# A decoder trunk on one core: the first half's inverses ahead of the convolution columns, the second half's convolution one stage sooner

## The chip, the core and the metric

The kernel runs on one core of a Trainium2 chip. The metric is the device time of one execution in microseconds; the time of a version is the median of several runs. Engines are called TensorE (PE in the rows; PEld is its loading of weights), VectorE (DVE), ScalarE (ACT), GpSimd (POOL) and SyncE (SP, which here only issues transfers).

## What is computed

One layer of a decoder with 1024 tokens of 1024 features, all in fp32. Three sub-layers, each `x <- x + RMSNorm_post(f(RMSNorm_pre(x)))`:

```python
# 1. mixer: one input projection p = h @ w_in, whose columns are split
y_conv = silu(layer_norm(causal_conv31(u * sigmoid(v)) ))   # 512 channels, 31 taps each
y_rwkv = rwkv7(...)                                         # 8 heads of 64, a recurrence over tokens
x = x + rms(concat(y_conv, y_rwkv) @ w_out)
# 2. cross attention of 4 heads into 256 memory tokens
x = x + rms(softmax(q @ km.T) @ vm @ wo)
# 3. SwiGLU
x = x + rms((silu(gu[:F]) * gu[F:]) @ w_down)
```

The recurrence per head keeps a 64 x 64 state S:

```python
s_kk = S @ kk_t
S = S * w_t - outer(s_kk, kk_t * a_t) + outer(v_t, k_t)
y_t = S @ r_t
```

## The kernel before, in words

The tokens are worked in two halves (b = 0 and 1) of 512. Every fp32 matmul is made of three: a weight tile of 128 x 1024 comes by SP into one of four `wraw` buffers (L174), ScalarE rounds it to a high part `whi` (L167) and VectorE takes the rest `wlo` (L168), each with two buffers; activations are split into `ahi` and `alo` in the same way. `mm3` (L190 to L192) does high times high, low times high and high times low, so 24 matmuls of 512 columns use one weight tile.

A half goes through these stages:

- **w_in_block** (L291): the input projection, panel by panel. Four panels are the convolution's (`conv_cols`); their gated result `evh` (L322) is stored to the DRAM array `hd`. The others (`mix_cols`) belong to the recurrence.
- **rwkv_prep** (L408): decays, keys and the products inside chunks of 64 tokens.
- **rwkv_values** (L558; its transposes are `psv`, L568) and **rwkv_inverse** (L578): a triangular inverse of 64 x 64 matrices, 32 x 32 blocks at first: 31 dependent steps of two VectorE instructions (L603, L604) on `Tt`. Through the DRAM arrays sc2 and sc3 the blocks come back in another layout, and matmuls `psx` (L623) and `pst2` (L630) finish `TT`.
- **rwkv_chain** (L634): 8 chunks, one after another. Each has five groups of 16 small matmuls on TensorE: psp (L671), psq (L676), psu (L681), pss (L686), psy (L696). Between them ScalarE copies (`pt`, `uv`) and VectorE updates the state `Sn` (L688 to L693). After two chunks `rwkv_out` (L707) normalizes the output with sums of heads on TensorE (`psbs`, L404) and a root on ScalarE and stores `Y` to `yd`.
- **conv** (L327): for each of four panels of channels a row `hin` of 542 tokens is loaded from `hd` (two buffers), ScalarE does the first tap (L340) and VectorE 30 more (L342), one instruction of 512 columns each, adding to `acc`: 120 taps a half. Then `conv_norm` (L347): layer norm and silu, the result stored to `yd`.
- **mix_out** (L796): `load_split` (L728) reads `yd` back and splits it, and 16 weight tiles make the output projection, `pst`.
- **attention** (L851), and **ffn** (L888).

`run` (L936) writes the stages in program order. `weave(main, side, rate)` (L51) mixes two generators by the microseconds that they yield; `self.fill(us)` lets the generator in `self.filler` write some of its work where the stage written now has gaps. Tile pools are stacks on two sides of the on-chip memory (`push`, `pop`); a pool pushed after another was popped takes over its space, and its first writers wait for that tile's last readers. The program is then put in order for each engine by the scheduler of the tile framework from this writing order and its own estimates, so the final order of an engine can be read only from the built program. An engine's list is fixed after that.

Before the change, in the first half: after the prep the convolution's four panels are projected; the convolution's pool is pushed under the inverse's, so its taps can run during the inverse; the recurrence is written, then the projection of the memory tokens (`memory_maps`), the norm of the second half and its first panels, woven with the convolution. Then mix_out and attention of the first half with the second half's other panels as filler. In the second half the recurrence has FFN0, the feed-forward block of the first half, as filler, woven with the second convolution.

Of the kernel before, what the change touches and what calls it, by code (L numbers as in the profile page):

```python
# [50 lines left out]
def weave(main, side, rate):  # L51

    lag = 0.0
    for us in main:
        yield us
        lag += us * rate
        while lag > 0.0:
            lag -= next(side, 1e9)
    drain(side)


def drain(*gens):
    for g in gens:
        for _ in g:
            pass


class Trunk:
# [867 lines left out]
    def run(self):  # L936
        tc = self.tc
        L, R = "left", "right"
        opened = {}

        def push(name, side):
            opened[name] = tc.tile_pool(name=name, bufs=1, side=side, reuse_waits="tile")
            return opened[name].__enter__()

        def pop(*names):
            for n in names:
                opened.pop(n).__exit__(None, None, None)


        self.fl = dict(res0=6.0, load0=6.0, soft0=5.0, res1=5.0, load1=16.0, soft1=0.0)  # L950
        self.filler = None
        self.credit = 0.0
        conv_cols, mix_cols = (4, 0, 6, 2), (20, 12, 8, 16, 14, 10, 18)

        edge = push("edge", R).tile([P, 56], F32, name="edge")
        self.nc.gpsimd.memset(edge, 0.0)

        a1 = push("a1", R)
        ev = push("ev", R)
        mk = push("mk", R)  # L960
        a0 = push("a0", R)
        h0, h1, mT = self.pairs(a0), self.pairs(a1), self.pairs(mk, MEM, "m")
        self.xn = 4
        self.xp = push("xa", L)
        self.normed(self.x, 0, (0, 4), h0, "g_mix", 2)
        drain(self.w_in_block(0, h0, ev, mix_cols[:1], 2))
        self.normed(self.mem, 0, (0, 2), mT, "g_mem", 2)
        pop("xa")
        self.lora_split(ev)
        self.nc.scalar.dma_start(out=self.hd[:, 0:CONVW - 1].rearrange("(j p) t -> p j t", p=P), in_=self.state[:, :, 0:CONVW - 1])  # L970
        drain(self.w_in_block(0, h0, ev, mix_cols[1:4]))
        pp = push("prep0", L)
        prep = self.rwkv_prep(0, pp)
        next(prep)
        drain(self.w_in_block(0, h0, ev, mix_cols[4:]))
        drain(prep)
        pop("prep0")
        drain(self.w_in_block(0, h0, ev, conv_cols))
        pop("a0")
        kv = push("kv", R)  # L980
        tp = push("tt0", L)
        TT = tp.tile([P, NCH * HP, CH], F32, tag="TT", name="TT")
        kp = push("conv0", L)
        pp = push("inv0", L)
        self.rwkv_values(0, pp)
        self.rwkv_inverse(0, pp, TT)
        self.xn = 2
        self.xp = push("xb", R)
        pop("inv0")

        gp = push("gn0", L)
        mp = push("mix0", L)
        self.rwkv_chain(0, mp, gp, TT)
        def next_norm():
            for t in range(0, 4, 2):
                self.normed(self.x, TB, (t, t + 2), h1, "g_mix", 2, (self.pd, "d"))
                yield 1.0 * 2
        maps = self.memory_maps(mT, ev, kv)
        w1 = self.w_in_block(1, h1, ev, conv_cols)
        main = chain(islice(maps, 16), next_norm(), islice(w1, 0), maps, w1)  # L1000
        drain(weave(main, self.conv(0, kp), 1.0))
        pop("mix0", "gn0", "conv0", "tt0", "xb", "kv", "mk")
        self.filler = self.w_in_block(1, h1, ev, mix_cols)

        yp = push("y0", L)
        a2 = push("a2", L)
        self.xn = 3
        self.xp = push("xc", R)
        ap = push("pc", R)
        drain(self.mix_out(0, a2, yp))  # L1010
        drain(self.attention(0, self.nextT, a2, yp, ap))
        self.fill(1e9)
        pop("pc", "xc")
        pop("ev", "a1")

        ya, ss = self.ya_tiles(yp), self.sums()
        fp = push("f0", L)
        self.filler = self.ffn(self.nextT, ya, ss, fp)
        pp = push("prep1", R)
        drain(self.rwkv_prep(1, pp))  # L1020
        pop("prep1")
        tp = push("tt1", R)
        TT = tp.tile([P, NCH * HP, CH], F32, tag="TT", name="TT")
        kp = push("conv1", R)
        pp = push("inv1", R)
        self.rwkv_values(1, pp)
        self.rwkv_inverse(1, pp, TT)
        pop("inv1")
        gp = push("gn1", R)
        mp = push("mix1", R)  # L1030
        self.rwkv_chain(1, mp, gp, TT)
        side = self.conv(1, kp)
        self.filler = weave(self.filler, side, 1.5)
        self.fill(270.0)
        drain(side)
        pop("mix1", "gn1", "conv1", "tt1")
        a3 = push("a3", R)
        y1 = push("y1", R)
        self.xn = 3
        self.xp = push("xd", R)  # L1040
        ap = push("pd1", R)
        drain(self.mix_out(1, a3, y1))
        drain(self.attention(1, self.nextT, a3, y1, ap))
        self.fill(1e9)
        drain(self.residual(0, ya, ss, 2, self.x2d, self.out, None, None))
        pop("pd1", "xd")
        pop("f0", "a2", "y0")

        ya, ss = self.ya_tiles(y1), self.sums()
        fp = push("f1", L)  # L1050
        self.wq, self.wbufs = push("we", L), 4
        self.xn = 5
        self.xp = push("xe", L)
        drain(self.ffn(self.nextT, ya, ss, fp))
        drain(self.residual(1, ya, ss, 2, self.x2d, self.out, None, None))
        pop("xe")
        pop("we")
        pop("f1")
        pop("y1", "a3", "edge")
# [54 lines left out]
```

## Time and profile before

| | |
|---|---|
| median of 3 runs | 1652.2 us (1651.72 to 1656.0) |
| the profiled execution | 1650.82 us, of it span 1649.1 us |
| TensorE busy | 1534.7 us (93%) |
| VectorE busy | 1065.5 us (65%) |
| ScalarE busy | 687.2 us (42%) |
| GpSimd busy | 51.0 us (3%) |
| mean granted clock of TensorE | 0.956 |

The page gives the busy time of each engine; a span is what lies between the first and the last instruction of the profiled execution. The busy shares are averages over stages of different kinds: the page's second part, the span in 40 slices, has TensorE at 9 tenths or more nearly everywhere, with dips at slices 5 to 7 (7 each), 10 and 11 (7 and 5) and 25 to 27 (7, 5 and 8). A slice is 41.2 us long. The last two dips are the recurrences of the two halves.

### The profile page before, as it was taken

Reading aid. Unit: us, or ns where it says so; the run is one execution under the profiler, and the core shown is the slowest. Engines: PE = TensorE matmul, PEld = TensorE weight load, DVE = VectorE, ACT = ScalarE, POOL = GpSimd, SP = SyncE. Lnnn points to the kernel's source line nnn. Section 1 sums busy time; section 2 is a strip of 40 time slices with the busy share of each in tenths; the row PEclk is TensorE's granted clock in tenths of the full one; section 3 lists DMA queues with packets and bytes.
Section 4 is the critical chain, followed back from the end, with each engine's and each line's share of the span. In section 5 each row is a group of like instructions: output and inputs, shape, how many; then the busy total and the mean of one; then the engine's idle time right before and its main releaser. Section 6 shows DMA issues by size and latency. Waiting matters only on the chain. (4 is left out here: it accounts for less than half of the span.)

```text
span 1649.1 us, 22648 instructions
## 1 busy us (share of the span) xinstructions
PE 1534.7 (93%) x8688; PEld 1258.7 (76%) x8688; DVE 1065.5 (65%) x1702; ACT 687.2 (42%) x1062; POOL 51.0 (3%) x102
## 2 busy tenths in 40 slices
PE   7999777997599999999999997589999999999997
PEld 6787766876487888787888886478887788888886
DVE  5678699986445646768799986446547634344445
ACT  5654454556434434654222246534435332222222
POOL 1000100000000000000000000001001100000000
PEclk9999997998599999999999997689999999999999
DMA  5576993846336235457833345445226623333321
GB/s 207 169 228 203 306 303 118 260 151 218 105 125 215 96 106 192 145 171 216 252 121 112 94 129 179 129 134 204 90 90 210 249 90 97 97 100 94 98 90 51
DMA packets 175643, 257.36 MB, mean 156 GB/s; under 512 B 68912, under 2 KB 110000, under 8 KB 175536
## 3 DMA queue, kind: packets, MB, share of 16 engines
q1 hardware_dynamic: 174576, 255.08, 48.8%
q8 instruction: 68, 1.11, 0.3%
q10 hardware_dynamic: 960, 0.85, 0.2%
q14 instruction: 39, 0.32, 0.1%
HBM read 196.58 MB, written 59.31 MB: 155 GB/s over the span
## 5 line engine op out<-in xcount | busy, mean ns | idle before, releaser
L167 ACT CAST whi<-wraw 128x1024 fp32r<-128x1024 f32 x256 | 268.5, 1050 | 593.3 <-PE psf L191 242.8
L168 DVE TENSOR_TENSOR wlo<-wraw,whi 128x1024 fp32r<-128x1024 f32 x256 | 313.0, 1224 | 282.6 <-ACT whi L167 281.3
L192 PE MATMUL psf<-ahi,wlo 128*128 128x512 f32 (+1 forms) x1200 | 456.0, 381 | 5.1 <-DVE wlo L168 5.0
L190 PE MATMUL psf<-ahi,whi 128*128 128x512 f32 (+1 forms) x1200 | 454.7, 380 | 5.6 <-ACT whi L167 4.6
L191 PE MATMUL psf<-alo,whi 128*128 128x512 f32 (+1 forms) x1200 | 455.2, 380 | 0.0
L190 PEld LDWEIGHTS psf<-ahi,whi 128*128 128x128 f32 x1200 | 228.1, 190 | 49.7 <-ACT whi L167 6.4
L192 PEld LDWEIGHTS psf<-ahi,wlo 128*128 128x128 f32 x1200 | 227.8, 190 | 49.6 <-DVE wlo L168 7.4
L191 PEld LDWEIGHTS psf<-alo,whi 128*128 128x128 f32 x1200 | 228.1, 190 | 42.0 <-issue 1.2
L342 DVE SCALAR_TENSOR_TENSOR acc<-hin,cols,acc 128x512 f32<-128x512 f32 x240 | 171.4, 749 | 1.7 <-ACT acc L340 1.6
L190 PE MATMUL pst<-whi,ahi 128*128 128x512 f32 x384 | 139.6, 403 | 16.8 <-ACT ahi L167 14.8
L191 PE MATMUL pst<-wlo,ahi 128*128 128x512 f32 x384 | 151.9, 397 | 0.0
L192 PE MATMUL pst<-whi,alo 128*128 128x512 f32 x384 | 147.1, 395 | 2.4 <-DVE alo L168 2.4
L191 PE MATMUL pst<-wlo,fhi 128*128 128x512 f32 x352 | 137.4, 391 | 0.0
L192 PE MATMUL pst<-whi,flo 128*128 128x512 f32 x352 | 134.3, 390 | 0.0
L190 PE MATMUL pst<-whi,fhi 128*128 128x512 f32 x352 | 133.3, 393 | 0.0
L190 PEld LDWEIGHTS pst<-whi,ahi 128*128 128x128 f32 x384 | 73.3, 192 | 33.0 <-ACT ahi L167 15.8
L192 PEld LDWEIGHTS pst<-whi,alo 128*128 128x128 f32 x384 | 72.6, 191 | 18.1 <-DVE alo L168 3.1
L191 PEld LDWEIGHTS pst<-wlo,ahi 128*128 128x128 f32 x384 | 73.9, 192 | 15.1
L191 PEld LDWEIGHTS pst<-wlo,fhi 128*128 128x128 f32 x352 | 66.1, 188 | 14.3 <-DVE wlo L168 0.4
L190 PEld LDWEIGHTS pst<-whi,fhi 128*128 128x128 f32 x352 | 65.8, 188 | 14.3 <-ACT whi L167 0.4
L192 PEld LDWEIGHTS pst<-whi,flo 128*128 128x128 f32 x352 | 66.1, 188 | 13.6
L230 POOL TENSOR_TENSOR rstd<-rstd,mhalf 128x1 f32<-128x1 f32 x50 | 35.4, 717 | 1314.1 <-DVE rstd L229 1304.6
(236 smaller groups left out, 1688.3 us busy)
## 6 DMA issues: line engine op xcount, KB each, us to landing
wraw<-in_w_gu_dram SPq DMA_DIRECT2D x88, 512.0 KB, 3.6
wraw<-in_w_in_dram SPq DMA_DIRECT2D x44, 512.0 KB, 4.0
wraw<-in_w_down_dram SPq DMA_DIRECT2D x44, 512.0 KB, 3.5
wraw<-in_wkv_dram SPq DMA_DIRECT2D x16, 512.0 KB, 5.4
am<-amd SPq DMA_DIRECT2D x16, 512.0 KB, 5.2
wraw<-in_w_out_dram SPq DMA_DIRECT2D x16, 512.0 KB, 3.9
wraw<-gd SPq DMA_DIRECT2D x16, 512.0 KB, 4.3
wraw<-vwd SPq DMA_DIRECT2D x16, 512.0 KB, 3.3
```

The source lines that it names most:

```text
L167: self.nc.scalar.copy(out=hi, in_=src)
L168: self.nc.vector.tensor_tensor(out=lo, in0=src, in1=hi.bitcast(F32), op=ALU.subtract)
L190: mm(ps, w[0], x[0], start=start, stop=False)
L191: mm(ps, w[0], x[1], start=False, stop=False)
L192: mm(ps, w[1], x[0], start=False, stop=stop)
L230: nc.gpsimd.tensor_tensor(r, r, self.mhalf, op=ALU.pow)
L342: nc.vector.scalar_tensor_tensor(out=a, in0=h[:, k:k + TB], scalar=w(k), in1=a, op0=ALU.mult, op1=ALU.add)
```

## The change

Three edits in `run`. First, the values and inverse of the first half (pools tt0 and inv0) are written ahead of the projection of the convolution's four panels, and the pool of the first convolution is pushed after inv0 has been popped, so that its tiles take over the inverse's space. Second, the pool of the second convolution is pushed before the first half's output projection, and that projection and the attention, as one generator, are woven with the second convolution at a rate of 0.7. Third, the second half's recurrence has only FFN0 as filler.

```diff
--- before.py
+++ after.py
@@ -975,18 +975,18 @@
         drain(self.w_in_block(0, h0, ev, mix_cols[4:]))
         drain(prep)
         pop("prep0")
-        drain(self.w_in_block(0, h0, ev, conv_cols))
-        pop("a0")
-        kv = push("kv", R)
+
         tp = push("tt0", L)
         TT = tp.tile([P, NCH * HP, CH], F32, tag="TT", name="TT")
-        kp = push("conv0", L)
         pp = push("inv0", L)
         self.rwkv_values(0, pp)
         self.rwkv_inverse(0, pp, TT)
+        drain(self.w_in_block(0, h0, ev, conv_cols))
+        pop("inv0", "a0")
+        kv = push("kv", R)
         self.xn = 2
         self.xp = push("xb", R)
-        pop("inv0")
+        kp = push("conv0", L)
 
         gp = push("gn0", L)
         mp = push("mix0", L)
@@ -1007,10 +1007,13 @@
         self.xn = 3
         self.xp = push("xc", R)
         ap = push("pc", R)
-        drain(self.mix_out(0, a2, yp))
-        drain(self.attention(0, self.nextT, a2, yp, ap))
+        kp = push("conv1", R)
+        def blocks():
+            yield from self.mix_out(0, a2, yp)
+            yield from self.attention(0, self.nextT, a2, yp, ap)
+        drain(weave(blocks(), self.conv(1, kp), 0.7))
         self.fill(1e9)
-        pop("pc", "xc")
+        pop("conv1", "pc", "xc")
         pop("ev", "a1")
 
         ya, ss = self.ya_tiles(yp), self.sums()
@@ -1021,7 +1024,6 @@
         pop("prep1")
         tp = push("tt1", R)
         TT = tp.tile([P, NCH * HP, CH], F32, tag="TT", name="TT")
-        kp = push("conv1", R)
         pp = push("inv1", R)
         self.rwkv_values(1, pp)
         self.rwkv_inverse(1, pp, TT)
@@ -1029,11 +1031,8 @@
         gp = push("gn1", R)
         mp = push("mix1", R)
         self.rwkv_chain(1, mp, gp, TT)
-        side = self.conv(1, kp)
-        self.filler = weave(self.filler, side, 1.5)
         self.fill(270.0)
-        drain(side)
-        pop("mix1", "gn1", "conv1", "tt1")
+        pop("mix1", "gn1", "tt1")
         a3 = push("a3", R)
         y1 = push("y1", R)
         self.xn = 3
```

The names in the rows below carry the program's buffer numbers: acc_2696 is the first half's convolution, acc_4446 the second's; hin_2697, 2937, 3212 and 3553 are the rows of the first's four panels, hin_4447, 4766, 5239 and 5436 those of the second's.

VectorE in the changed program, in the midst of the first half's recurrence (L724 is its output):

```order
L240 SCALAR_TENSOR_TENSOR yrr_2418<-ysq_2410,yrr_2418 128x512
L351 TENSOR_TENSOR lnsa_3819<-acc_2696 128x512
L342 SCALAR_TENSOR_TENSOR acc_4446<-hin_4447,cols_77,acc_4446 128x512
L342 SCALAR_TENSOR_TENSOR acc_2696<-hin_3212,cols_77,acc_2696 128x512
L724 TENSOR_TENSOR Y_2250<-Y_2250,yrr_2418 128x512
L342 SCALAR_TENSOR_TENSOR acc_4446<-hin_4447,cols_77,acc_4446 128x512
L342 SCALAR_TENSOR_TENSOR acc_2696<-hin_3553,cols_77,acc_2696 128x512
```

Before, only the first convolution's taps stood here; the second's begin beside its third and fourth panels, and go on alternating with them until the first convolution's taps end.

VectorE at the first alo of the first half's output projection; alo comes from araw, the row read back from `yd`. Before:

```order
L721 TENSOR_SCALAR yrr_2650<-psbs_2647 128x512
L239 SCALAR_TENSOR_TENSOR ysq_2642<-ysq_2642,yrr_2650 128x512
L240 SCALAR_TENSOR_TENSOR yrr_2650<-ysq_2642,yrr_2650 128x512
L724 TENSOR_TENSOR Y_2558<-Y_2558,yrr_2650 128x512
L724 TENSOR_TENSOR Y_2558<-Y_2558,gt_2639 128x512
L724 TENSOR_TENSOR Y_2558<-Y_2558,bv_2638 128x512
L168 TENSOR_TENSOR alo_4329<-araw_4326,ahi_4328 128x512
```

And in the changed program (L383 is the last row of the first convolution's norm):

```order
L383 SCALAR_TENSOR_TENSOR acc_2696<-lnth_4061,acc_2696 128x512
L342 SCALAR_TENSOR_TENSOR acc_4446<-hin_5239,cols_77,acc_4446 128x512
L342 SCALAR_TENSOR_TENSOR acc_4446<-hin_5436,cols_77,acc_4446 128x512
L383 SCALAR_TENSOR_TENSOR acc_2696<-lnth_4067,acc_2696 128x512
L342 SCALAR_TENSOR_TENSOR acc_4446<-hin_5239,cols_77,acc_4446 128x512
L342 SCALAR_TENSOR_TENSOR acc_4446<-hin_5436,cols_77,acc_4446 128x512
...
L168 TENSOR_TENSOR alo_4332<-araw_4329,ahi_4331 128x512
```

The recurrence's last output stood ahead of the alo; now it is the end of the first convolution's norm and taps of the second convolution's third and fourth panels (four more of the same two kinds at the line of dots), and the last wlo ahead of this place stands 155 rows earlier.

TensorE in the second half's recurrence, ahead of the second output projection (pst_9750). Before, its last rows; psp to psbs of the five chunks ahead of these read alike:

```order
L405 MATMUL psbs_7450<-yhl_7447,blk_105 128x512
L671 MATMUL psp_7465<-uv_7380,am_7376 64x64 x8
L676 MATMUL psq_7475<-qt_7312,Sn_7425 64x64 x8
L681 MATMUL psu_7486<-pt_7464,TT_6636 64x64 x8
L686 MATMUL pss_7497<-uv_7380,bt_7378 64x64
L696 MATMUL psy_7509<-am_7376,uv_7380 64x64
L686 MATMUL pss_7497<-uv_7380,bt_7378 64x64 x7
L696 MATMUL psy_7509<-am_7376,uv_7380 64x64 x7
L404 MATMUL psbs_7528<-yhl_7525,blk_105 128x512
L405 MATMUL psbs_7528<-yhl_7525,blk_105 128x512
L190 MATMUL pst_9750<-whi_9756,ahi_9598 128x512
L191 MATMUL pst_9750<-wlo_9757,ahi_9598 128x512
```

In the changed program, the last chunk's pss and psy (psf_9517 and psf_9553 are products of FFN0):

```order
L191 MATMUL psf_9517<-alo_6171,whi_9513 128x512
L192 MATMUL psf_9517<-ahi_6170,wlo_9514 128x512
L190 MATMUL psf_9553<-ahi_6156,whi_9549 128x512
L191 MATMUL psf_9553<-alo_6157,whi_9549 128x512
L686 MATMUL pss_7688<-uv_7571,bt_7569 64x64 x8
L696 MATMUL psy_7700<-am_7567,uv_7571 64x64 x8
L192 MATMUL psf_9553<-ahi_6156,wlo_9550 128x512
```

The recurrence's groups stood one behind another; now each stands between matmuls of FFN0, of which 94 follow the last psy.

## Rows read from the trace of the kernel before

**Rows 1.** Each engine's busy time by stretch; the columns stand in its first line.
```profile
core 0: us, PE busy (x) PEld busy (x) DVE busy (x) ACT busy (x) POOL busy (x), PEclk, DMA share, GB/s
192.00:350.00 158.00, 126.69 (x1025) 107.36 (x1024) 150.79 (x261) 71.41 (x111) 1.97 (x2) 0.90 0.68 217
350.00:440.00 90.00, 65.93 (x697) 52.28 (x695) 53.08 (x96) 54.29 (x86) 0.00 (x0) 0.79 0.54 173
447.00:1009.00 562.00, 560.84 (x2968) 456.10 (x2968) 406.24 (x649) 232.36 (x352) 14.41 (x30) 0.99 0.49 153
1009.00:1079.00 70.00, 38.89 (x494) 31.87 (x493) 37.04 (x71) 37.02 (x61) 0.00 (x0) 0.60 0.49 144
```

**Rows 2.** TensorE's waits from 1000 to 1085 us: total, times, longest.
```profile
PE pst L190 <- ACT ahi L167: 8.9, 1, 8.9
PE pss L686 <- ACT uv L683: 8.3, 6, 2.5
```

**Rows 3.** TensorE's timeline at the second recurrence: start, duration, instruction, idle before.
```profile
1007.95 0.64 PE L696 MATMUL psy<-am,uv 128*64 128x64 f32 x16
1008.52 0.50 PE L191 MATMUL pst<-wlo,fhi 128*128 128x512 f32 x1
1008.85 0.40 PE L192 MATMUL pst<-whi,flo 128*128 128x512 f32 x1
...
1081.87 0.39 PE L190 MATMUL pst<-whi,ahi 128*128 128x512 f32 x1
```

**Rows 4.** VectorE's timeline: inverse and recurrence of both halves, first projection.
```profile
186.54 1.23 DVE L168 TENSOR_TENSOR wlo<-wraw,whi 128x1024 fp32r<-128x1024 f32 x1 [1.28 <-ACT whi L167]
189.42 1.23 DVE L168 TENSOR_TENSOR wlo<-wraw,whi 128x1024 fp32r<-128x1024 f32 x1 [1.32 <-ACT whi L167]
195.85 1.22 DVE L168 TENSOR_TENSOR wlo<-wraw,whi 128x1024 fp32r<-128x1024 f32 x1
...
312.02 0.23 DVE L604 TENSOR_TENSOR Tt<-Tt,tm 128x31 f32<-128x31 f32 x1
318.23 4.72 DVE L342 SCALAR_TENSOR_TENSOR acc<-hin,cols,acc 128x512 f32<-128x512 f32 x7
322.87 1.22 DVE L168 TENSOR_TENSOR wlo<-wraw,whi 128x1024 fp32r<-128x1024 f32 x1
351.52 0.42 DVE L688 TENSOR_TENSOR Sn<-pss,state 128x256 f32<-128x256 f32 x1
...
445.99 2.58 DVE L168 TENSOR_TENSOR alo<-araw,ahi 128x512 fp32r<-128x512 f32 x4 [2.35 <-DMA yd<-Y]
...
956.52 0.21 DVE L604 TENSOR_TENSOR Tt<-Tt,tm 128x31 f32<-128x31 f32 x1
991.80 0.42 DVE L688 TENSOR_TENSOR Sn<-pss,Sn 128x256 f32<-128x256 f32 x1
```

**Rows 5.** TensorE's timeline at the first half's output projection.
```profile
441.58 0.63 PE L190 MATMUL pst<-whi,ahi 128*128 128x512 f32 x1
...
453.29 0.40 PE L190 MATMUL pst<-whi,ahi 128*128 128x512 f32 x1
...
455.81 0.39 PE L192 MATMUL pst<-whi,alo 128*128 128x512 f32 x1
```

**Rows 6.** TensorE's waits from 175 to 460 us.
```profile
PE pstr L270 <- DVE xt L256: 9.1, 2, 8.0
```

**Rows 7.** VectorE's groups, 350 to 440 us: count, busy, mean, idle before.
```profile
L688 DVE TENSOR_TENSOR Sn<-pss,Sn 128x256 f32<-128x256 f32 x7 | 3.0, 422 | 8.3 <-PE pss L686 8.2
L383 DVE SCALAR_TENSOR_TENSOR acc<-lnth,acc 128x512 f32<-128x512 f32 x4 | 2.8, 691 | 2.1 <-ACT acc L382 2.1
L239 DVE SCALAR_TENSOR_TENSOR ysq<-ysq,yrr 128x512 f32<-128x512 f32 x3 | 2.1, 692 | 12.9 <-ACT ysq L238 12.9
L351 DVE TENSOR_TENSOR lnsq<-lnsq 128x512 f32<-128x512 f32 x3 | 2.1, 689 | 1.4 <-ACT lnsq L366 1.4
L372 DVE TENSOR_SCALAR lnrs<-psln 128x512 f32<-128x512 f32 x1 | 0.7, 693 | 2.2 <-PE psln L370 2.2
```

## The prediction

> **What bounds the kernel now.** The views were read in this order.
>
> First the busy time of each engine by stage [rows 1]. Between 447 and 1009 us TensorE is busy for 560.84 of 562 us. That is the stretch from the first half's output projection to the end of the filler in the second half's recurrence, and nothing on VectorE can shorten or lengthen it as long as TensorE is fed: VectorE works 406.24 us there. Around it lie two stretches where TensorE is not the bound: 192 to 440 us (126.69 + 65.93 of 248 us) and 1009 to 1079 us (38.89 of 70).
>
> Second, the list of TensorE's waits from 1000 us on, and third its timeline there [rows 2, 3]. The last filler matmul of the feed-forward block starts at 1008.85, the output projection waits 8.9 us for its ahi and reaches its 13th matmul at 1081.87, and between them the last six of eight recurrence steps stand alone; six times they wait for uv.
>
> Third, VectorE's timeline at the first half's inverse, at its end, the first state update and the first alo of the output projection [rows 4], and TensorE's timeline at that projection [rows 5].
>
> A difference of 0.3% (5 us) is what the runs can tell from no change. The sum is made against the profiled execution: span 1649.1, its own time 1650.82, so 1.7 us lie around the span, and it stands 1.4 us under the median of 1652.2.
>
> **Second half: what is gained.** The change takes the second convolution out of the second recurrence's filler. By the order of TensorE, all eight steps then stand between matmuls of the feed-forward block, and behind the last step's matmuls 94 of 512 columns remain before the output projection. The lonely stretch goes; the steps' own matmuls stay. Its length: full-speed matmuls start 0.228 us apart (453.29 to 455.81 are eleven of them [rows 5]), so filler would have gone on at 1009.08; the projection's first 12 matmuls are done when the 13th starts at 1081.87, as if it had begun at full speed at 1081.87 - 12 x 0.228 = 1079.13 [rows 3]. That is 70.0 us. Six steps still have to be done: a group of 16 small matmuls takes 0.64 us at full clock, of which 0.57 until the next instruction starts (1007.95 to 1008.52 [rows 3]); five groups a step, so 6 x 5 x 0.57 = 17.1 us, and four pairs of psbs, two 512-column matmuls each, at an estimated 0.65 us, 2.6 us: 19.7 us. Gain 70.0 - 19.7 = **50.3 us**. The projection's 8.9 us wait for ahi [rows 2] is covered: 94 x 0.228 = 21.4 us of matmuls stand there now. I keep 1 us for leftover waits: **-49 us**. Bounds: -50 (no wait) to -40 (the wait for ahi comes back whole).
>
> Taking 120 taps off VectorE beside FFN0 gives nothing by itself, since TensorE was full there [rows 1].
>
> **First half: what is lost.** Nothing before psv, the transposes of the values, moves on TensorE, so 192 us is common. From there on I follow VectorE, which takes its instructions in the order written.
>
> Inverse. The 31 steps now run without taps between them, but the 11 weight splits wlo among them are paced by matmuls: 186.54 to 189.42, 2.88 us apart [rows 4]. From the split at 195.85 that is 11 x 2.86 = 31.5 us, to 227.3; the last steps and 8 transposes with their alo bring some 5 us, and the next norm's xt, for which the transposes waited 8.0 us before [rows 6], may be late too, half of it counted: Tt is ready at **236** instead of 312.02. From Tt to the first state update it took 351.52 - 312.02 = 39.5 us in the first half and 991.80 - 956.52 = 35.3 in the second [rows 4]. I take 35.3, since VectorE has few other rows in that piece now: the update comes at **271**, between 262 (227.3 + 35.3) and 279 (240 + 39.5). That is 80 us earlier than before.
>
> But what used to fill VectorE in the inverse, the first convolution's taps, has not been done yet: its pool now lies over the inverse's buffers, and only 5 of its 120 taps stand ahead of the update. And the second convolution's taps do not stand beside the output projection, as the change says: by VectorE's order they begin where the first convolution's third and fourth panels begin and alternate with them. Between the update and the first alo of the projection stand 115 taps of the first convolution, **99 of the second**, 23 wlo, and about 100 others of the chain, its outputs, the layer norm. Seven taps in a row run from 318.23 until the next instruction at 322.87, 0.663 each [rows 4]: 214 x 0.663 = 141.9. A wlo takes 1.22; (4.72 - 4.64) of overlap off [rows 4], it costs 1.135: 26.1. The others, in the same way 0.61 for one of 512 columns and 0.34 to 0.43 for the smaller, 50.8. Sum **218.8 us**, of which the 99 taps are 65.6.
>
> Idle time. In 350:440, where these same chain and norm rows ran before, VectorE was busy 53.08 of 90 us. The layer norm's own waits were 1.4 (lnsq), 2.2 (lnrs) and 2.1 (acc) us; the chain's seven updates waited 8.3, and three of the four outputs 12.9 for the rsqrt on ScalarE [rows 7]. Taps now stand in most of these gaps. Bounds: nothing, or all, 5.7 + 8.3 + 4/3 x 12.9 = 31 us. I take the norm's 5.7 whole, since only a few taps stand at the end, and a third of the rest: **14 us**, which also has to pay for the reloads of hin (two buffers for each convolution, both in use).
>
> So the first alo comes at 271 + 218.8 + 14 = **504** instead of 445.99 [rows 4]. Before, 24 matmuls were done at 453.29, as if begun at full speed at 453.29 - 24 x 0.228 = 447.8 [rows 5], 1.8 us after the alo. TensorE has had no wlo for 155 rows of VectorE when it resumes, and the matmuls after such a pause took 0.63 each instead of 0.40 [rows 5]: I take 3 us. 504 + 3 - 447.8 = **+59 us**. Through the projection VectorE now has 21 taps and the second layer norm as well: by the same prices 60.6 us of work beside its first 12 weight tiles, 12 x 24 x 0.228 = 66 us of matmuls. I count **+2** (0 to 6).
>
> Queues. The second convolution's hin loads and hd stores now stand on SP's queue between the weight loads of the first half's last tiles; one that waits for a free hin buffer holds the wraw loads behind it. Four raw buffers lie between, and TensorE has slack there anyway: nothing. ScalarE does the four first taps and the second norm earlier; it is busy 54.29 of 90 us in 350:440 and 232.36 of 562 in the long stretch [rows 1]: nothing beyond the waits counted. POOL does nothing that moves.
>
> The Trainium skill, Perfetto Trace Analysis, section Tensor Engine Instruction, calls VectorE and ScalarE "strict FIFO": no alo passes the taps. The trace agrees as far as it goes: the seven taps in a row from 318.23 keep back the next wlo [rows 4].
>
> **Sum.** +59 + 2 - 49 = +12: span 1661, time 1650.8 + 12 = **1663 us**, 11 above the median.
>
> **The rivals.**
>
> *The overlap works (faster).* The 99 taps fall where VectorE is half idle, beside projection and attention. Then the alo comes 65.6 us sooner: +59 - 66 = -7, with -49 and +2 a change of -54, **1597 us**. Against it: the order is fixed. For it speaks the Trainium skill, Perfetto Trace Analysis, Optimization Strategy: "performance may be improved by interleaving those regimes", which is what the words of the change describe. No row shows VectorE taking a later instruction first. Chance 0.02.
>
> *VectorE hardly waits (faster).* The update comes at 262, as the narrower matmuls of the memory maps between psx and pss let the chain through, and the idle time is 5: alo at 486, +41 + 2 - 49 = -6 to, with no idle at all, -11: **1640 to 1645**. It decides from an alo at about 487. For: TensorE has little to do from 272 on but feed the chain. Against: 31 us of waits before. Chance 0.14.
>
> *The two cancel (no change).* Alo between 488 and 498: **1647 to 1657**. Chance 0.17.
>
> *It is worse than forecast (slower).* The reloads of hin and the chain's round trips stop VectorE as much as before (31 us), or the steps inside FFN0 make its matmuls wait, as the wait for uv was up to 2.5 us each [rows 2]; eight times two such waits are up to 20 us: **1675 to 1690**. Chance 0.20. The forecast itself, 1657 to 1675, has 0.47.
>
> **Numbers.** Faster 0.16, same 0.17, slower 0.67. Range 1640 to 1685: it leaves out the first rival and the ends of the second and the last.
>
> **What would show it.** In the changed profile: Tt ready near 236 and the first state update near 271; in some 100 us ahead of the output projection VectorE above 90% busy with taps of both accumulators and TensorE nearly idle, at half its clock; the first alo near 504, the projection waiting for it. Between 450 and the end TensorE full; no lonely steps before the second projection, and that stretch 50 us shorter. I am wrong if the first alo comes before 488, if TensorE is busy during the taps, or if FFN0 grows by waits of the chain.

## The result, and the profile after

The changed kernel takes **1667.03 us** (median of 4 runs, 1666.04 to 1667.81) against 1653.27 for the kernel before (4 runs). The ratio is 1.0076, 95% interval 1.0064 to 1.0088: slower by some 13 us (12.6 by the ratio, 13.8 by the medians), where 11 were forecast. The profiled execution has a span of 1665.1 us, 16.0 more than the one before.

VectorE's timeline of the changed kernel, at the places of [rows 4] (start, duration, instruction, idle before):

```profile
238.74 0.20 DVE L604 TENSOR_TENSOR Tt<-Tt,tm 128x31 f32<-128x31 f32 x1
274.66 0.42 DVE L688 TENSOR_TENSOR Sn<-pss,state 128x256 f32<-128x256 f32 x1
...
463.01 0.69 DVE L351 TENSOR_TENSOR lnsb<-acc 128x512 f32<-128x512 f32 x1
...
497.76 0.68 DVE L383 SCALAR_TENSOR_TENSOR acc<-lnth,acc 128x512 f32<-128x512 f32 x1
...
502.34 1.28 DVE L168 TENSOR_TENSOR alo<-araw,ahi 128x512 fp32r<-128x512 f32 x2
```

The inverse is done at 238.74 instead of 312.02, the first state update comes at 274.66 instead of 351.52, and still the first alo of the output projection comes at 502.34 instead of 445.99. From 463.01, where the layer norm sums the last two panels of the first convolution, to 497.76, its last row, 35 us pass.

What filled that time, by engine, and the long stretch behind it; the columns are as in [rows 1]:

```profile
core 0: us, PE busy (x) PEld busy (x) DVE busy (x) ACT busy (x) POOL busy (x), PEclk, DMA share, GB/s
272.00:380.00 108.00, 103.92 (x900) 87.55 (x900) 99.37 (x153) 56.24 (x88) 0.00 (x0) 0.97 0.70 228
380.00:500.00 120.00, 23.47 (x174) 16.09 (x170) 119.90 (x190) 31.56 (x44) 0.00 (x0) 0.59 0.14 44
504.00:1095.00 591.00, 584.71 (x3460) 472.96 (x3459) 375.91 (x611) 264.56 (x407) 15.82 (x30) 0.99 0.51 159
```

In 380:500 VectorE is busy 119.90 of 120 us, TensorE 23.47, at a mean granted clock of 0.59, near the lower of its two levels. In 272:380 both work: TensorE 103.92 and VectorE 99.37 of 108 us. TensorE's timeline shows what it waited for in 380:500, and how the projection then began:

```profile
465.67 2.08 PE L357 MATMUL psln<-lnsa,ones 128*128 128x512 f32 x2 [49.17 <-DVE lnsa L351]
...
477.89 2.07 PE L370 MATMUL psln<-lnsq,ones 128*128 128x512 f32 x2 [10.14 <-DVE lnsq L351]
...
501.51 0.79 PE L190 MATMUL pst<-whi,ahi 128*128 128x512 f32 x1 [21.55 <-ACT ahi L167]
...
506.77 0.39 PE L190 MATMUL pst<-whi,ahi 128*128 128x512 f32 x1
...
509.50 0.39 PE L190 MATMUL pst<-whi,ahi 128*128 128x512 f32 x1
```

That is 49 us for the convolution's sum, 10 for the sum of squares, 21.6 for the projection's ahi. The 25th matmul of the projection starts at 509.50: as if begun at full speed at 509.50 - 24 x 0.2275 = 504.0, against 447.8 before [rows 5]. That is **56.2 us later**.

In the second half the lonely steps are gone. Two places of TensorE's timeline there, a chain step between matmuls of FFN0, and the beginning of the second output projection:

```profile
1060.80 0.39 PE L192 MATMUL psf<-ahi,wlo 128*128 128x512 f32 x1
1061.12 0.69 PE L671 MATMUL psp<-uv,am 128*64 128x64 f32 x16
1061.74 0.68 PE L676 MATMUL psq<-qt,Sn 64*64 64x64 f32 x16
1062.35 0.50 PE L190 MATMUL psf<-ahi,whi 128*128 128x512 f32 x1
1062.68 0.40 PE L191 MATMUL psf<-alo,whi 128*128 128x512 f32 x1
...
1094.80 0.39 PE L192 MATMUL pst<-whi,flo 128*128 128x512 f32 x1
1095.02 0.39 PE L190 MATMUL pst<-whi,ahi 128*128 128x512 f32 x1
```

The projection follows FFN0 without a gap, at 1095.0. From one projection to the other it is 591 us, before 1079.1 - 447.8 = 631.3: **40.3 us less**. Behind 1095.0 the span goes on for 570.1 us, before 570.0. So 56.2 - 40.3 + 0.1 = 16.0, the difference of the spans.

### The profile page after: what moved, and what is told of

The parts are those of the page before. It is cut to its first block, busy times and chain, and to the rows that moved or that the text cites. A ratio compares the mean times of both kernels' runs of the same rounds, so it can differ in the third digit from the quotient of the medians.

```text
span 1665.1 us, 22614 instructions
## 1 busy us (share of the span) xinstructions
PE 1513.3 (91%) x8688; PEld 1239.4 (74%) x8688; DVE 1068.6 (64%) x1702; ACT 686.9 (41%) x1062; POOL 50.8 (3%) x102
## 4 chain that ended last, share of the span: by engine, by line
PE 81%; DVE 11%; DMA 4%; ACT 3%; issue 1%; SPq 0%; POOL 0%; DVEq 0%; POOLq 0%; ACTq 0%
PE psf L190 14%; PE psf L192 14%; PE psf L191 14%; PE pst L190 10%; PE pst L191 10%; PE pst L192 10%; DVE acc L342 6%; PE psg L514 1%; DVE wlo L168 1%; PE pstr L270 1%; PE pspr L428 1%; DMA gd<-evg 1%; ACT whi L167 1%; DMA xt<-in_x_dram 1%; DMA hin<-hd 1%
## 5 line engine op out<-in xcount | busy, mean ns | idle before, releaser
L190 PEld LDWEIGHTS psf<-ahi,whi 128*128 128x128 f32 x1200 | 227.7, 190 | 47.2 <-ACT whi L167 4.8
L342 DVE SCALAR_TENSOR_TENSOR acc<-hin,cols,acc 128x512 f32<-128x512 f32 x240 | 166.9, 746 | 4.0 <-ACT acc L340 3.8
L190 PE MATMUL pst<-whi,ahi 128*128 128x512 f32 x384 | 138.6, 400 | 22.7 <-ACT ahi L167 21.6
L903 DVE TENSOR_TENSOR ya<-pst,ya 128x512 f32<-128x512 f32 x80 | 54.2, 688 | 43.7 <-PE pst L192 43.5
L921 DVE SCALAR_TENSOR_TENSOR ftg<-ftg,psf 128x512 f32<-128x512 f32 x44 | 30.2, 685 | 76.4 <-PE psf L192 76.1
```

Of the source, the lines that this page charges most:

```text
L190: mm(ps, w[0], x[0], start=start, stop=False)
L342: nc.vector.scalar_tensor_tensor(out=a, in0=h[:, k:k + TB], scalar=w(k), in1=a, op0=ALU.mult, op1=ALU.add)
L903: nc.vector.tensor_tensor(out=y, in0=ps, in1=y, op=ALU.add)
L921: nc.vector.scalar_tensor_tensor(out=tg, in0=tg, scalar=0.5, in1=pu, op0=ALU.mult, op1=ALU.mult)
```

## The experiments

Each kernel is described by three times of its profiled execution. S1 is the start of the first projection as if at full speed, worked out as above from its 25th matmul; then the time from S1 to the same point S2 of the second projection; then the rest of the span. The ratios are to the kernel before, on the same chip. In the experiments the kernel before took 1656.6 to 1657.2 us, 3 to 4 more than above. The five kernels that have the first half of before (inv1_first, b_gate, b_gate12, b_gate2, b_gate12_al) came to S1 between 452.5 and 456.2 there, so first halves are compared with 453 and not with 447.8. S1 of one execution is uncertain by some us: hold and hold_al, whose engines have the same order, differ by 6.5, and hold_al's profiled execution (1645.5) lies 4 us under its median.

| kernel | S1 | S1 to S2 | rest | median us | ratio (95%) |
|---|---|---|---|---|---|
| before | 447.8 | 631.3 | 570.0 | | 1 |
| changed | 504.0 | 591.0 | 570.1 | 1667.0 | 1.0076 (1.0064 to 1.0088) |
| a_only | 456.5 | 633.9 | 570.0 | 1662.0 | 1.0032 (1.0019 to 1.0044) |
| b_only | 487.8 | 592.9 | 570.1 | 1653.6 | 0.9980 (0.9967 to 0.9992) |
| hold | 462.0 | 609.6 | 580.1 | 1653.6 | 0.9984 (0.9970 to 0.9998) |
| inv1_first | 452.5 | 628.5 | 569.9 | 1652.2 | 0.9973 (0.9961 to 0.9985) |
| b_gate | 453.4 | 610.0 | 580.2 | 1645.0 | 0.9918 (0.9902 to 0.9933) |
| hold_fill | 475.1 | 599.8 | 580.2 | 1655.5 | 0.9983 (0.9971 to 0.9994) |
| a_fill | 468.9 | 623.9 | 570.0 | 1662.9 | 1.0032 (1.0017 to 1.0046) |
| bi_fill | 467.4 | 632.3 | 561.5 | 1664.2 | 1.0042 (1.0024 to 1.0060) |
| b_gate12 | 452.7 | 611.1 | 578.1 | 1642.6 | 0.9907 (0.9884 to 0.9931) |
| b_gate2 | 453.0 | 635.9 | 578.1 | 1668.9 | 1.0080 (1.0054 to 1.0106) |
| hold_al | 455.5 | 610.1 | 578.1 | 1649.6 | 0.9950 (0.9931 to 0.9970) |
| b_gate12_al | 456.2 | 605.1 | 579.6 | 1639.9 | 0.9893 (0.9874 to 0.9913) |

### The two halves of the change apart

**a_only**: the first edit alone.

```diff
-        drain(self.w_in_block(0, h0, ev, conv_cols))
...
         self.rwkv_inverse(0, pp, TT)
+        drain(self.w_in_block(0, h0, ev, conv_cols))
+        pop("inv0", "a0")
...
+        kp = push("conv0", L)
```

> First edit alone (the first half's inverse ahead of the convolution's panels, its pool freed before the first convolution's); the second convolution stays in the second recurrence. Theory T (the loss of the first half is the second convolution's 99 taps ahead of the first alo): without them the alo comes 65.6 us sooner than the changed kernel's 502.3, at about 437, 9 us ahead of the 446 of before; the second half as before: about 1644 us, 1653 at most if TensorE sets the end there. Rival R1 (the loss comes from the inverse that VectorE now runs without taps to fill it): the first half stays late by 25 us or more and nothing is gained behind it: 1678 or more.

Measured 1.0032, some 5 us slower; S1 is 3.5 us later than 453, no more than equal first halves differ by. Both theories missed. Without the 99 taps S1 does come sooner (456.5 instead of 504), but not by 65.6 us. VectorE's timeline of a_only at its layer norm:

```profile
426.87 0.69 DVE L351 TENSOR_TENSOR lnsa<-lnsa,lnsb 128x512 f32<-128x512 f32 x1
429.73 2.48 DVE L359 SCALAR_TENSOR_TENSOR acc<-psln,acc 128x512 f32<-128x512 f32 x4 [2.16 <-PE psln L357]
...
437.75 0.69 DVE L372 TENSOR_SCALAR lnrs<-psln 128x512 f32<-128x512 f32 x1 [2.17 <-PE psln L370]
441.74 0.69 DVE L239 SCALAR_TENSOR_TENSOR lnt<-lnt,lnrs 128x512 f32<-128x512 f32 x1 [3.30 <-ACT lnt L238]
...
449.21 1.40 DVE L383 SCALAR_TENSOR_TENSOR acc<-lnth,acc 128x512 f32<-128x512 f32 x2 [1.58 <-ACT acc L382]
454.79 1.29 DVE L168 TENSOR_TENSOR alo<-araw,ahi 128x512 fp32r<-128x512 f32 x2 [4.17 <-ACT ahi L167]
```

From the sum at 426.87 to the alo at 454.79 are 28 us, of which VectorE is busy 12.5 and waits 15.4: for psln on TensorE, for squares, root and the last scaling on ScalarE, for the row to come back and be rounded. This chain has to be gone through whether taps stand in it or not. In the changed kernel taps of the second convolution filled its gaps, so some 15 of their 65.6 us cost nothing.

**b_only**: the second and third edit, without the first.

```diff
+        kp = push("conv1", R)
+        def blocks():
+            yield from self.mix_out(0, a2, yp)
+            yield from self.attention(0, self.nextT, a2, yp, ap)
+        drain(weave(blocks(), self.conv(1, kp), 0.7))
...
-        self.filler = weave(self.filler, side, 1.5)
```

> The second convolution moved to the first output projection and attention, the first inverse as before. Theory T: its taps stand ahead of the first alo here too, by VectorE's order 113 rows more than before; 75 us less what VectorE had idle there (up to 40): the alo comes at 480 to 505, and with 40 us gained behind it 1645 to 1672, about 1655. Rival R1: the first half is as before, the alo near 446, and the 40 us stay: about 1613.

```profile
485.84 0.68 DVE L168 TENSOR_TENSOR alo<-araw,ahi 128x512 fp32r<-128x512 f32 x1
```

The alo comes at 485.84, S1 35 us later than 453, and S1 to S2 is 38.4 us shorter: within what theory T expected, and R1 is out. In its trace 108 taps of the second convolution run ahead of the alo, in the changed kernel 99. The taps ahead of the alo delay the projection also where the inverse is untouched, and the gain of the second half belongs to these edits alone. The two halves of the change don't simply add: apart +0.3% and -0.2%, together +0.8%. The 99 taps cost 47.5 us of S1 where the inverse was moved (504.0 against a_only's 456.5), the 108 only some 35 where it wasn't.

### The taps behind the alo

**hold**: the changed kernel; GpSimd writes a one-column tile `gate` from the first convolution's result, and from `gate` a column of the second's first two hin rows ahead of their load, which overwrites it. So the load, and the taps behind it, wait for that result.

```diff
             nc.sync.dma_start(out=self.yd[j * P:(j + 1) * P, t0:t0 + TB], in_=a)
+            if b == 0 and j == 3:
+                nc.gpsimd.tensor_tensor(out=self.gate, in0=a[:, 0:1], in1=a[:, 0:1], op=ALU.mult)
...
+            if b == 1 and j < 2:
+                nc.gpsimd.tensor_tensor(out=h[:, 0:1], in0=self.gate, in1=self.gate, op=ALU.mult)
             nc.sync.dma_start(out=h, in_=self.hd[j * P:(j + 1) * P, t0:t0 + TB + CONVW - 1])
...
+        self.gate = opened_edge.tile([P, 1], F32, name="gate")
```

> The changed kernel, but the second convolution's first two rows can only be loaded when the first convolution's result is complete, so its taps stand behind the first alo. Theory T: the first half as with the first edit alone (alo near 437), the second half as in the changed kernel, and at most 10 us of waits where 120 taps stand beside the projection and attention: 1604 to 1614. Rival R1: the first half stays late: 1655 or more.

```profile
460.31 1.30 DVE L168 TENSOR_TENSOR alo<-araw,ahi 128x512 fp32r<-128x512 f32 x2 [4.47 <-ACT ahi L167]
```

The first alo comes at 460.31 instead of 502.34: holding back the second convolution's taps, with nothing else moved, brings 42 us back in the first half. But 19 are lost between the projections (609.6 against 591.0), where TensorE now idles 16.8 us instead of 6.3, and 10 behind the second. The time, 1653.6, is neither T's 1604 to 1614 nor R1's 1655 or more: R1 is out by the first half, and T had the place of the taps right but not the price behind it.

**b_gate**: the same on b_only, with the gate written from the recurrence's last output `Y` instead.

```diff
         nc.sync.dma_start(out=self.yd[DR:, t0:t0 + GW].rearrange("(h p) t -> p h t", p=P), in_=Y)
+        if t0 + GW == TB:
+            nc.gpsimd.tensor_tensor(out=self.gate, in0=Y[:, HP - 1, GW - 1:GW], in1=Y[:, HP - 1, GW - 1:GW], op=ALU.mult)
```

> The second convolution moved, the first inverse as before, and the second convolution's first two rows loaded only when the first recurrence's last output is complete, so its taps stand behind the first alo. Theory T (what costs is where the taps stand: ahead of the alo they cost, behind it they don't): the projection begins as before, near 448 by full speed instead of 488 in the run without this gate; behind it the 38 us of the second half's gain less some 18 us of waits beside the attention, as in the run with the hold: 1630 to 1642 us. Rival R2 (VectorE's sum of work is the bound, the place doesn't matter): 1650 or more.

0.9918: 12 to 14 us faster than the kernel before, with the first half as before (453.4) and 21 us less between the projections. The time is 3 us above the range given, but on a chip on which the kernel before took 4 us more, and R2 is out: against b_only only the place of the taps was changed (by the gate's few GpSimd instructions), and that brought 34 us in the first half. What TensorE waits for between 470 and 700 us in b_gate:

```profile
PE pstr L270 <- DVE ya L256: 12.4, 2, 6.2
PE pst L190 <- ACT pb L868: 2.3, 1, 2.3
PE psf L190 <- ACT pb L868: 2.1, 1, 2.1
```

That is some 17 us, mostly where the projection's result is normalized and transposed for the attention: short steps of VectorE on which TensorE hangs, with taps among them.

**b_gate12** and **b_gate2** put half of the taps, or all, behind that place: `gate2` is written from the first normalized activations of the attention. b_gate2 also writes the convolution beside the attention alone, at a rate of 1.5, instead of beside projection and attention at 0.7.

```diff
+            if b == 0 and gi == 0:
+                z = self.nextT[KT - 1][1][:, 0:1].bitcast(F32)
+                self.nc.gpsimd.tensor_tensor(out=self.gate2, in0=z, in1=z, op=ALU.mult)
...
+                z = self.gate if j < 2 else self.gate2
```

> As the run with the gate on the recurrence's last output (ratio 0.992), but the second convolution's third and fourth panels are loaded only when the first normalized activations of the attention are complete. Theory T2 (the 18 us still lost beside the attention are TensorE's two waits of 6 us for ya at the change from projection to attention, and the slow clock after them, since taps stand among VectorE's short steps there): half the taps stand behind that place, the waits shrink from 12.4 to under 5 us and 8 to 15 us are gained: ratio 0.983 to 0.987. Rival (the taps only move the waits to the next such place, behind the attention): ratio 0.99 to 0.995.

> The same with all four panels of the second convolution behind the attention's first normalized activations. Theory T2: no tap stands at the change from projection to attention, its waits go as in the kernel before; the taps end 18 us later and 80 us of them lie beside attention and the second preparation: ratio 0.980 to 0.987. Rival: taps and layer norm now run into the second change and the second preparation, and TensorE waits there: ratio 0.99 or more.

b_gate12 can't be told from b_gate, and theory T2 missed: the wait for ya is 10.6 us there, where under 5 were expected. b_gate2 lost 25 us between the projections, and with them all that the second half had gained; of its waits between the projections:

```profile
PE psln L372 <- DVE lnsq L353: 11.3, 1, 11.3
PE pst L190 <- ACT pb L871: 5.1, 1, 5.1
PE pstr L270 <- DVE ya L256: 0.5, 1, 0.5
```

The wait for ya is gone, but TensorE now stands 11.3 us for the layer norm's sum. That is the rival's way, waits further on instead of these. Between the projections TensorE idles 30.9 us, 12 more than b_gate's 19.0. And the granted clock falls behind the wait for the sum: 0.51 from 712 to 754 us, where b_gate has 1.00. The 28 us that TensorE works there would take half as long at the upper level, so the clock costs an estimated 14. Together that is the loss.

### Is it the taps that left, or the recurrence that moved?

**inv1_first**: the kernel before, with the second convolution's pool pushed behind the second inverse instead of ahead of it.

```diff
-        kp = push("conv1", R)
         pp = push("inv1", R)
...
         pop("inv1")
+        kp = push("conv1", R)
```

> The kernel before with one move in the second half: the second convolution's pool is pushed after the second inverse's is popped, so its taps can't stand among the inverse's 31 steps but stand beside the recurrence. Theory A (the second half gained because the second convolution's taps left that stage): the taps are still there, so nothing is gained: 1650 to 1656. Theory B (it gained because the inverse is done sooner without taps among its steps, and the recurrence then starts while filler is left): by TensorE's order all eight steps stand in the filler, so 40 us are gained: about 1613.

0.9973, 4.5 us. The steps do stand in the filler, but of the 40 us only this comes. TensorE's waits between 980 and 1100 us:

```profile
PE pst L190 <- ACT ahi L167: 17.2, 1, 17.2
PE psln L357 <- DVE lnsa L351: 10.2, 1, 10.2
PE psln L370 <- DVE lnsq L351: 5.9, 1, 5.9
```

In place of the lonely steps TensorE waits 33 us for the second convolution's layer norm and the projection's activations behind it. So theory B has the mechanism of the stretch right and is still wrong on the time: with the taps left in this stage, the convolution ends late instead of the recurrence. For the gain the recurrence had to start while filler was left, and the taps had to be out of this stage as well.

### Filler for the layer norm

**hold_fill**, **a_fill**, **bi_fill**: hold, a_only and again a_only with `self.fill(30.0)` ahead of the first projection; bi_fill also takes inv1_first's edit and `self.fill(300.0)` for 270, which puts more of FFN0 ahead of S2 (its rest is 8.5 us shorter).

> The changed kernel with the hold, and 30 us of the second half's input projection written ahead of the output projection, beside the first convolution's layer norm. Theory N (the first edit costs because the layer norm, 28 us from its first sum to the alo, stands alone ahead of the projection): those 28 us of TensorE's idle are filled, and 20 to 28 us are gained on the run with the hold alone (ratio 0.998): about 1630 us. Rival: the projection and the attention lack the filler that was taken from them and wait as much: 1650 or more.

> The first edit alone, and the same 30 us of filler ahead of the output projection. Theory N: 20 to 28 us better than the first edit alone (ratio 1.003): 1630 to 1640 us. Rival: as the first edit alone, 1655 or more.

> Both inverses ahead of their convolutions' taps (first edit, and the second convolution's pool pushed after the second inverse's), 30 us of filler ahead of the first output projection and 30 us more of FFN0 (300 instead of 270) in the second recurrence. Theory N: both layer norms stand beside matmuls, the recurrence's steps too, so the 70 us of the second half's lonely stretch shrink to the steps' own 20 and the first half gains 15: about 1590 to 1605 us. Rival (VectorE's sum of work is the bound in both stages): 1630 or more.

None gained: hold_fill and a_fill have the ratios of hold and a_only, and bi_fill, whose two inverses were not tried together without filler, is no faster than a_only. TensorE's timeline of hold_fill:

```profile
445.36 2.08 PE L359 MATMUL psln<-lnsa,ones 128*128 128x512 f32 x2 [13.60 <-DVE lnsa L353]
...
453.38 2.07 PE L372 MATMUL psln<-lnsq,ones 128*128 128x512 f32 x2 [5.95 <-DVE lnsq L353]
...
472.75 0.80 PE L190 MATMUL pst<-whi,ahi 128*128 128x512 f32 x1 [17.30 <-ACT ahi L167]
```

The filler was put in order ahead of the norm's sums, not among them, so the 17.3 us wait stays as it was (17.4 in hold); S1 is 13 us later in hold_fill and the time from S1 to S2 10 us shorter. Whether filler that stands behind psln would help wasn't tried.

### The 10 us behind the second projection

**hold_al** and **b_gate12_al**: the gates 64 bytes wide instead of 4.

```diff
-        self.gate = opened_edge.tile([P, 1], F32, name="gate")
+        self.gate = opened_edge.tile([P, 16], F32, name="gate")[:, 0:1]
```

> The run with the hold, in which only the one-column tile that carries the hold is now 16 columns wide (64 bytes a partition instead of 4), so the tiles behind it in the on-chip memory lie as in the kernel before; the order of every engine is the same. Theory P (the place of the tiles slows TensorE: in the five runs with this tile 347 of 512-column matmuls were done in 80 us of the last feed-forward block where the kernel before did 354, at the same granted clock): 354 again, the stretch behind the second projection 570 us instead of 580, and some 5 to 10 us less ahead of it: ratio 0.986 to 0.990 instead of 0.998. Rival (the slower matmuls come from something else in those runs, the chip's state for one): ratio 0.998, 347 matmuls.

> The run with two gates, with both carrying tiles 16 columns wide, the order of every engine the same. Theory P: 354 matmuls in 80 us, ratio 0.979 to 0.984 instead of 0.991. Rival: ratio 0.991, 347 matmuls.

Theory P, as put, fell: 347 matmuls in 80 us again, and the rest of the span stays at 578 to 580. But the expectation is wrong in that the wider tile puts the tiles behind it where they lie in the kernel before: a wider tile can only move them further. So the place as such was not tested. The intervals of the ratios touch or overlap those of the narrow gates. **b_gate12_al**, at 1639.9 us, is the fastest of all and beats both kernels: 0.9893, 0.9874 to 0.9913; b_gate and b_gate12 can't be told from it.

## Why the prediction was right

- *Tt at 236, the update at 271*: 238.74 and 274.66. The length of the tail held (35.9 us from Tt to the update, 35.3 taken). That Tt came so near to 236 is in part luck: the pace of 2.88 us held from 218.75 to 230.26, but nine wlo came, not eleven, with none between 195.89 and 208.86, and the last at 233.60 instead of 227.3; the wait for the next norm's xt, of which 4 us were counted ahead of Tt, fell behind it.
- *218.8 us of VectorE and 14 of idle up to the first alo*: 219.0 of work and 8.7 of idle, 227.7 together instead of 232.8. The price of the queue was right; the idle was smaller and lay elsewhere, 8.6 us up to 380 and 0.1 behind it, where I had expected the layer norm to stop VectorE. The taps filled its gaps. So the update 3.7 us late and the idle 5.3 us short offset each other, and the alo came at 502.34, forecast 504.
- *+3 us for the slow clock*: 1.7 (504.0 - 502.34), where before it was 1.8. TensorE's matmuls took 0.63 us up to the 12th and 0.39 from the 13th on (506.77); before, the full pace came with the 25th [rows 5].
- *+59 us*: 56.2.
- *-49 us and +2*: together -40.3 instead of -47, the term that was mis-sized, by 7 us. A chain step costs more between other matmuls than my 5 x 0.57: in the timeline above psp and psq take 0.62 and 0.61 until the next start, and on either side of them a 512-column matmul is followed after 0.32 and 0.33 instead of 0.228 us. With psu apart, and pss with psy, there are three such places a step: 0.62 + 0.61 + 0.61 + 0.51 + 0.57 + 3 x 0.2 = 3.5 instead of 2.85, 4 us more in six steps. The four psbs pairs, an estimate of 0.65 each, took 0.47, 0.7 us less together. And TensorE waits for the normalized row of the projection's result, with the 21 taps still standing there; of its waits from 500 to 1140 us:

```profile
PE pst L190 <- ACT ahi L167: 21.6, 1, 21.6
PE pstr L270 <- DVE ya L256: 5.9, 1, 5.9
```

  The first is the one ahead of the projection. Between the projections TensorE idles 6.3 us, where before it idled 1.2 from 447.8 to the lonely stretch: 5.1 more, for which the +2 and the 1 us of leftover waits stood, so 2 us too little. The rest, some 1 us, is what the clock cost behind that wait: the five matmuls from 579.64 on start 0.45 us apart on the mean instead of 0.228.
- *The overlap works (1597)*: refuted by the order and by b_only against b_gate: the taps that stand ahead of the alo in b_only cost 34 us there. The rule that VectorE is "strict FIFO" (the Trainium skill, Perfetto Trace Analysis, Tensor Engine Instruction) agrees with both. What the Trainium skill says in Optimization Strategy of the same page, that "performance may be improved by interleaving those regimes", did not come true for the change as it was made (1.0076); its second and third edit alone gave 0.9980, and with the taps held behind the alo 0.9918.
- Where the reasoning was too simple: it counted the 99 taps at 65.6 us of the loss. By hold (S1 462.0) and hold_al (455.5) against the changed kernel (504.0) they cost 42 to 48. The rest stays as the first edit's own: the layer norm's chain, 28 us with little to do for TensorE or VectorE, now stands at the end of the half, while before it ran beside the recurrence [rows 7]. Nothing of this changes the sum, since the taps and the gaps that they fill were both in it.

## What to carry to other kernels

Work that is moved beside a stage "with room" goes where the scheduler finds it ready, not where it was written: look in the built order for what stands ahead of the first instruction that the next stage waits for, and price that queue row by row. If it must stand behind, a data dependency of one column does it: here it turned the changed kernel's loss of 0.8% into a gain of 0.2 to 0.5% (hold, hold_al), and with the first edit left out a gain of 0.2% into one of 0.8 to 1.1%. A serial chain such as a layer norm at the end of a stage costs its whole length, and work that fills it is free only up to the idle time in it (15.4 of 28 us here).

## What the runs showed of the hardware that was not expected

In all seven kernels with a gate tile the last feed-forward block runs slower at the same granted clock. TensorE in 1420:1500, busy time, matmuls, clock; the changed kernel, then hold (all seven have 347):

```profile
1420.00:1500.00 80.00, 80.00 (x355) 1.00 0.32 99
```

```profile
1420.00:1500.00 80.00, 80.00 (x347) 1.00 0.30 98
```

355 matmuls against 347 in 80 full us, 2.3%. By groups in 1340:1420, first the changed kernel, then b_gate (count, busy us, mean ns of one, idle before):

```profile
L190 PE MATMUL psf<-ahi,whi 128*128 128x512 f32 x71 | 27.6, 389 | 0.0
L190 PE MATMUL pst<-whi,fhi 128*128 128x512 f32 x48 | 18.7, 389 | 0.0
```

```profile
L190 PE MATMUL psf<-ahi,whi 128*128 128x512 f32 x84 | 33.2, 396 | 0.0
L190 PE MATMUL pst<-whi,fhi 128*128 128x512 f32 x32 | 12.5, 389 | 0.0
```

In this block only psf is slower, 396 against 389 ns. Its 512-column operand is the activations, in a pool on the right side of the on-chip memory, which lies behind the gate tile; pst, whose 512-column operand is the weights on the left side, keeps 389. The block has 1056 psf, so 7 ns each are 7.4 of the 8 to 10 us.

The same kernels have psf with activations on either side. In 0:400 these are the input projection's, on the right, in 800:900 FFN0's, on the left. The changed kernel, then b_gate, first 0:400, then 800:900:

```profile
L191 PE MATMUL psf<-alo,whi 128*128 128x512 f32 x240 | 94.5, 394 | 0.0
L191 PE MATMUL psf<-alo,whi 128*128 128x512 f32 x240 | 96.5, 402 | 0.0
...
L191 PE MATMUL psf<-alo,whi 128*128 128x512 f32 x85 | 33.3, 392 | 0.0
L191 PE MATMUL psf<-alo,whi 128*128 128x512 f32 x76 | 29.7, 391 | 0.0
```

On the right 402 against 394 ns, on the left 391 against 392. So within one kernel the slowing goes with the side on which the activations lie. It reaches the first half as well: 720 such psf in 0:400 at 8 ns are some 6 us, part of which the waits there can hide. That speaks for the place of the tiles. But gate tiles of 64 and 128 bytes a partition in all were as slow as 4 and 8, and no run moved those pools without a gate. The kernel before has a tile of its own ahead of them, `edge`, of 56 columns, which is written once and never read; why it has that size is not on record. What about the place slows the matmuls stays open.
